# A state-space stage: constants loaded in an earlier block, and two GpSimd products given to VectorE

## The chip, the cores and the metric

One core of one Trainium2 chip runs the whole program. The time is the device time of one execution in microseconds. TensorE (PE; its weight loads are PEld) multiplies into PSUM, VectorE (DVE), ScalarE (ACT) and GpSimd (POOL) work on tiles in SBUF, and transfers are issued from the queues of SyncE (SP), ACT and POOL. Each engine runs its own instructions in order and waits at an instruction until what it needs is there.

## The reference, cut to what matters

The input is 512 tokens of 1024 columns. Two layers of a first block (a gated short convolution beside a rotary retention) come first; then 16 meta tokens are put ahead, and a state-space layer (SSD), an MLP, an attention layer and another MLP follow, 528 tokens each. Of the state-space layer, with 32 heads in 8 groups and chunks of 128 tokens:

```python
z, xbc, dt = jnp.split(h @ w_in, ...)
xbc = jax.nn.silu(causal_depthwise_conv_2(xbc, conv_w, conv_b))
dt = jax.nn.softplus(dt + dt_bias)
a = -jnp.exp(a_log)
a_cs = jnp.cumsum(dt * a)                            # in each chunk
y_diag = einsum(cb * exp(a_cs_l - a_cs_s), x * dt)   # in a chunk
y_off = einsum(c * exp(a_cs), state before the chunk)
g = rms_norm((y + x * d_skip) * silu(z)) * norm_g    # in each group
out = g @ w_out
```

All is float32. To keep its precision a product is made of three matmuls: each factor is a high part (a cast, by ACT) and a low part (the rest, by DVE or POOL).

## The kernel before, in words

**Weights.** `Stream` (lines 27 to 78) loads all weights in one order, 1 MB of 1024 rows and 256 columns at a time, from SP's queue into `wraw`, of which there are two. ACT casts four pieces of it to `whi` (line 65) and DVE subtracts to get `wlo` (line 66); there are two of each. A weight's `whi` buffer comes free when TensorE has done the weight two places before it, so ACT can cast the next weight only while TensorE works on the one in between. In the first block TensorE works a weight off in 11.1 us.

**First block, convolution half** (from line 455). For each of four parts p the weights come in the order c, x, b, z. DVE takes the sums out of PSUM (`cR` for c and x, `t` for b, `s` for z), ACT makes silu of `s`, DVE `t*s`, and `split` (line 247) forms the high part `mh_c` (ACT) and the low part `ml_c` (DVE) of the mixed tile.

**State-space stage** (from line 659). Its pool `sp` takes the SBUF space of the first block's pool. Before its first weight stand its constants: `dcol` (two transfers of 64x16 single floats, each 8 bytes behind the last, line 665), `e1`, `dtb` (line 672) and `ea` (line 674), all transfers from POOL's queue, and exp(`ea`) on ACT (line 675). The taps of its convolution are halved in `vec` on DVE (line 691). `steps` (line 692) makes dt and the running sums; only its line 722 reads `ea`. Then, for each of 8 groups, five chunks c: `cb` and `M` (DVE, lines 798 and 804), the decayed C `eb` (exp on ACT, line 810, times C on POOL, line 811), matmuls with `M` (line 818) and `eb` (line 820), the states `pv` (POOL line 833, DVE line 834) and the gated tile `gz` (DVE line 839, POOL line 841). At a group's end `gz` is normed (line 879) and split; the low part `ml_s` is POOL's in groups 0 to 6, DVE's in group 7 (line 881). The matmuls of the next weights stand between those of a chunk.

**Order.** A scheduler orders each engine's instructions when the program is built, by its own estimate of when each could start; it moves them across the statements of the source, as long as what they depend on allows. So an instruction's place in the source isn't its place on its engine.

Of the kernel before, what the change touches and what calls it, by code (L numbers as in the profile page):

```python
# [9 lines left out]
F32 = mybir.dt.float32  # L10
# [3 lines left out]
AF = mybir.ActivationFunctionType  # L14
ALU = mybir.AluOpType
PSUM = bass.MemoryType.PSUM

P = 128
# [3 lines left out]
T2 = SEQ + META  # L22
# [57 lines left out]
def build(ctx, tc, a):  # L80
    nc = tc.nc
    V = nc.vector
# [108 lines left out]
    cols = cp.tile([P, 4], F32, name="cols")  # L191
    Rx = cp.tile([P, T2], F32, name="Rx")
    vec = cp.tile([P, 3 * P], F32, name="vec")
    xres = cp.tile([P, 8, T2], F32, name="xres")
    V_PRE, V_POST, V_CW, V_LNM, V_LNF = 0, 16, 32, 80, 96
    V_SCW, V_SCB, V_SNG, V_QA, V_KVA = 128, 256, 288, 304, 307
# [51 lines left out]
    def split(dst, src, cs, eng=V):  # L248
        h, l = dst
        nc.scalar.copy(h[:, cs], src)  # L250
        eng.tensor_tensor(l[:, cs], src, h[:, cs].bitcast(F32), ALU.subtract)
# [31 lines left out]
    with ExitStack() as c1:  # L283
# [171 lines left out]
        for l in range(2):  # L455

            mixc = []
            for p in range(4):
                cR = [tmp(f"cR{l}{p}{n}") for n in range(2)]
                if p == 0:  # L460
                    for _, os_, u, pss in duo([(l, "c", 0), (l, "x", 0)], X, META, load_x if l == 0 else None):
                        for n in range(2):
                            V.tensor_tensor(cR[n][:, os_], pss[n], (RR, cR[n])[u][:, os_], ALU.mult)
                else:
                    for n, ps in dense((l, "c", p), X):
                        V.tensor_tensor(cR[n], ps, RR, ALU.mult)
                    for n, ps in dense((l, "x", p), X):
                        V.tensor_tensor(cR[n], ps, cR[n], ALU.mult)
                ts = []
                for n in range(2):  # L470
                    j = 2 * p + n
                    u = cR[n]
                    t = tmp(f"t{l}{j}")
                    wc = [gcol(V_CW, (l * 3 + q) * 8 + j) for q in range(3)]
                    nc.scalar.activation(t, u, AF.Identity, scale=wc[2])
                    V.scalar_tensor_tensor(t[:, 1:], u[:, :-1], wc[1], t[:, 1:], ALU.mult, ALU.add)
                    V.scalar_tensor_tensor(t[:, 2:], u[:, :-2], wc[0], t[:, 2:], ALU.mult, ALU.add)
                    ts.append(t)
                for n, ps in dense((l, "b", p), X):
                    V.tensor_tensor(ts[n], ps, ts[n], ALU.mult)  # L480
                    V.tensor_tensor(ts[n], ts[n], R, ALU.mult)
                for n, ps in dense((l, "z", p), X):
                    s = tmp(f"s{l}{p}{n}")
                    V.tensor_tensor(s, ps, R, ALU.mult)
                    nc.scalar.activation(s, s, AF.Silu)
                    V.tensor_tensor(ts[n], ts[n], s, ALU.mult)
                    m = mix_tile(f"c{l}{p}{n}")
                    split(m, ts[n], MS)
                    mixc.append(m)
                if l == 0 and p == 0:  # L490
                    late_vectors()
                    rotary_tables()
                if p == 3:
                    c_ = tmp(f"crot{l}")
                    nc.sync.dma_start(c_, rot[0])
                    V.tensor_tensor(CR, c_, R, ALU.mult)
                    s_ = tmp(f"srot{l}")
                    nc.sync.dma_start(s_, rot[1])
                    V.tensor_tensor(SR, s_, R, ALU.mult)

                    for b in range(4):
                        nc.tensor.transpose(C0[:, P * b : P * b + P], R[:, P * b : P * b + P], ident)
                    V.tensor_copy(Rt, C0[:, 0 : 4 * P : P])
# [148 lines left out]
    with ExitStack() as c2:  # L652
# [7 lines left out]
        small = {n: sp.tile([P, 5, 32], F32, name=n) for n in ("dt", "acs", "wd", "cdec")}  # L660
        dt, acs, wd, cdec = (small[n] for n in ("dt", "acs", "wd", "cdec"))
        acsD = tc.dram_tile([32, T2], F32, name="acsD")
        dcol = sp.tile([P, 16], F32, name="dcol")
        for i in range(2):
            nc.gpsimd.dma_start(
                dcol[64 * i : 64 * i + 64, :],
                a["ssd_d_2"][0].rearrange("(j two) -> two j", two=2)[i : i + 1].partition_broadcast(64))
        e1 = sp.tile([P, 32], F32, name="e1")
        V.memset(e1, 0.0)
        V.memset(e1[:, 0:1], 1.0)  # L670
        dtb = sp.tile([32, 1], F32, name="dtb")
        nc.gpsimd.dma_start(dtb, a["ssd_dt_bias_2"].rearrange("o h -> h o"))
        ea = sp.tile([P, 32], F32, name="ea")
        nc.gpsimd.dma_start(ea, a["ssd_a_log_2"].partition_broadcast(P))
        nc.scalar.activation(ea, ea, AF.Exp)
        def conv_silu(ps, j, tag, name):

            u = tmp(f"u{name}")
# [9 lines left out]
            V.scalar_tensor_tensor(t, u, 1.0, t, ALU.add, ALU.mult)  # L688
            return t

        V.tensor_scalar(vec[:, V_SCW : V_SNG + 16], vec[:, V_SCW : V_SNG + 16], 0.5, None, ALU.mult)
        def steps():

            w = ws.next("dt")
            ps = acc2()[:, :, :HW]
            mm3([(ps[:32, i], HS[i]) for i in range(2)], w, slice(0, 32), X, 8)
            dT = tmp("dT")[:32]
            V.tensor_tensor(halves(dT), ps[:32], halves(Rx)[:32], ALU.mult)
            nc.scalar.activation(dT, dT, AF.Identity, bias=dtb)
            for c, (t0, W) in enumerate(CH):  # L700
                nc.tensor.transpose(D0[:W, 32 * c : 32 * c + 32], dT[:, t0 : t0 + W], ident[:32, :32])
            f = [tmp(f"sf{i}", "sz", 3)[:, :160] for i in range(3)] + [tmp("sf3", "rb", 1)[:, :160]]
            x_, e_, s_, q_ = f
            V.memset(x_[:, :32], 0.0)
            V.tensor_copy(x_[:META, :32], D0[:META, :32])
            V.tensor_copy(x_[:, 32:], D0[:, 32:160])
            V.scalar_tensor_tensor(e_, x_, -1.0, x_, ALU.mult, ALU.max)
            nc.scalar.activation(e_, e_, AF.Exp, scale=-1.0)

            V.tensor_scalar(s_, e_, 2.0, None, ALU.add)  # L710
            V.reciprocal(s_, s_)
            V.tensor_tensor(s_, s_, e_, ALU.mult)
            V.tensor_tensor(e_, s_, s_, ALU.mult)
            V.tensor_scalar(q_, e_, 1.0 / 17.0, None, ALU.mult)
            for n in range(15, 1, -2):
                V.scalar_tensor_tensor(q_, q_, 1.0 / n, e_, ALU.add, ALU.mult)
            V.scalar_tensor_tensor(q_, q_, 1.0, s_, ALU.add, ALU.mult)
            V.tensor_scalar(x_, x_, 0.0, None, ALU.max)
            dtf = dt.rearrange("p c h -> p (c h)")
            V.scalar_tensor_tensor(dtf, q_, 2.0, x_, ALU.mult, ALU.add)  # L720
            V.tensor_scalar(dt[:, 0], dt[:, 0], cols[:, 2:3], None, ALU.mult)
            V.scalar_tensor_tensor(e_.rearrange("p (c h) -> p c h", c=5), dt, -1.0,
                                   ea.unsqueeze(1).to_broadcast([P, 5, 32]), ALU.mult, ALU.mult)
            cs_ps = D0
            nc.tensor.matmul(cs_ps[:, :160], tri, e_, start=True, stop=True)
            nc.tensor.matmul(cs_ps[:, 160:320], ones, e_, start=True, stop=True)
            acf, wdf, cdf = (t.rearrange("p c h -> p (c h)") for t in (acs, wd, cdec))
            V.tensor_copy(acf, cs_ps[:, :160])
            V.tensor_tensor(wdf, cs_ps[:, 160:320], acf, ALU.subtract)
            nc.scalar.activation(wdf, wdf, AF.Exp)  # L730
            V.tensor_tensor(wdf, wdf, dtf, ALU.mult)
            nc.scalar.activation(cdf, cs_ps[:, 160:320], AF.Exp)
            aT = tmp("aT")[:32]
            for c, (t0, W) in enumerate(CH):
                tp = (D0, D1)[c % 2][:32, :W]
                nc.tensor.transpose(tp, acs[:W, c, :], ident[:W, :W])
                V.tensor_copy(aT[:, t0 : t0 + W], tp)
            nc.gpsimd.dma_start(acsD, aT)
# [19 lines left out]
        for g in range(8):  # L758
# [24 lines left out]
            for c, (t0, W) in enumerate(CH):  # L783
# [24 lines left out]
                if c > 0:  # L808
                    eb = sp.tile([P, 4, P], F32, tag="eb", name=f"eb{nm}", bufs=2)
                    nc.scalar.activation(eb, ab, AF.Exp)  # L810
                    nc.gpsimd.tensor_tensor(eb, eb, Cs[:, ts_].unsqueeze(1).to_broadcast([P, 4, P]), ALU.mult)
                for n in range(2):
                    for cross in range(2 if c > 0 else 1):
                        for i in range(2):
# [63 lines left out]
            for n in range(2):  # L878
                V.scalar_tensor_tensor(gz[n], gz[n], gcol(V_SNG, 2 * g + n), rb, ALU.mult, ALU.mult)
                m = mix_tile(f"s{g}{n}")  # L880
                split(m, gz[n], slice(0, T2), nc.gpsimd if g < 7 else V)
                mix.append(m)
        Xn, sums = out_pass(2, mix)
        X = Xn
# [82 lines left out]
    with c4:  # L967
# [55 lines left out]
        for i in range(2):  # L1023
            o = side[i][:3, :HW]
# [359 lines left out]
```

## Time and profile before

| | |
|---|---|
| time, median of 3 runs (lowest to highest) | 2577.65 us (2577.57 to 2577.69) |
| profiled execution, its own time | 2570.25 us |
| its span | 2568.5 us |
| PE busy | 2502.8 us, 97% |
| DVE busy | 1476.5 us, 57% |
| ACT busy | 996.3 us, 39% |
| POOL busy | 258.1 us, 10% |
| mean granted clock of TensorE | 0.993 |

Busy is the time in which an engine had at least one instruction in work; matmuls overlap, so TensorE's busy share says little about its pace. The page's slices show TensorE at nine tenths or more nearly throughout; the slice from 1027 to 1092 us is at seven tenths, and there alone the granted clock falls to 0.7. That is the start of the state-space stage, which lasts to about 1538 us.

### The profile page before, as it was taken

What the parts mean: (1) busy time and instruction counts of PE and PEld (TensorE: products, weight loads), DVE (VectorE), ACT (ScalarE), POOL (GpSimd) and SP (SyncE); (2) the same over time, 40 slices, a digit from 0 to 9 for tenths busy, and PEclk for the clock granted to TensorE, in tenths of its full rate; (3) what the DMA queues carried; (4) which work ended last, traced back from release to release, by engine and by line L of the source; (5) the groups of instructions that cost most, each with busy time, mean ns of one, the idle gap of its engine ahead of it and who ended that gap; (6) DMA issues with size and microseconds to landing.
All of it is one profiled execution on the core that took longest, in us unless ns stands there. A gap on an engine that the chain in (4) does not pass through costs nothing.

```text
span 2568.5 us, 40249 instructions
## 1 busy us (share of the span) xinstructions
PE 2502.8 (97%) x16657; PEld 2212.7 (86%) x16657; DVE 1476.5 (57%) x2844; ACT 996.3 (39%) x2162; POOL 258.1 (10%) x254
## 2 busy tenths in 40 slices
PE   8999999999999999799999999999999999999999
PEld 7888888888888888699999999999997666799898
DVE  6743555564435456588848875434455765644443
ACT  4322333432223344365535543323335764423321
POOL 1000000100000002153413430000011000100000
PEclk9999999999999999799999999999999999999999
DMA  4333222223332321433333223232322121223322
GB/s 141 107 99 107 66 83 88 76 71 96 107 94 78 91 81 54 64 100 95 94 96 93 79 82 106 83 99 83 99 69 71 52 61 43 90 85 96 99 91 74
DMA packets 213383, 220.88 MB, mean 86 GB/s; under 512 B 8796, under 2 KB 203469, under 8 KB 213200
## 3 DMA queue, kind: packets, MB, share of 16 engines
q1 hardware_dynamic: 208512, 207.50, 26.4%
q0 software_dynamic: 4208, 10.68, 2.4%
q8 instruction: 130, 2.13, 0.3%
q14 instruction: 53, 0.43, 0.1%
q10 hardware_dynamic: 480, 0.13, 0.0%
HBM read 215.46 MB, written 2.83 MB: 85 GB/s over the span
## 4 chain that ended last, share of the span: by engine, by line
PE 89%; DVE 4%; ACT 3%; DMA 1%; POOL 1%; issue 1%; POOLq 0%; ACTq 0%; DVEq 0%
PE pb L222 57%; PE main L222 10%; PE main L229 8%; PE pb L229 4%; PE side L1217 1%; PE side L1230 1%; PE side L818 1%; DMA ea<-ssd_a_log 1%; PE main L1223 1%; PE side L827 1%; POOL sums L260 1%; DVE wlo L66 1%; PE side L543 1%; PE side L561 1%; DVE M L804 1%
## 5 line engine op out<-in xcount | busy, mean ns | idle before, releaser
L65 ACT CAST whi<-wraw 128x512 fp32r<-128x512 f32 (+2 forms) x721 | 408.0, 621 | 906.3 <-PE pb L222 567.2
L66 DVE TENSOR_TENSOR wlo<-wraw,whi 128x512 fp32r<-128x512 f32 (+2 forms) x721 | 491.3, 722 | 192.7 <-ACT whi L65 191.7
L222 PE MATMUL pb<-xh_n,whi 128*128 128x264 f32 (+3 forms) x1264 | 348.6, 325 | 16.7 <-ACT whi L65 13.9
L222 PE MATMUL pb<-xh_n,wlo 128*128 128x264 f32 (+3 forms) x1264 | 357.3, 328 | 0.0
L222 PE MATMUL pb<-xl_n,whi 128*128 128x264 f32 (+3 forms) x1264 | 349.1, 325 | 0.0
L222 PEld LDWEIGHTS pb<-xh_n,whi 128*128 128x128 f32 (+1 forms) x1264 | 215.5, 190 | 35.9 <-ACT whi L65 14.1
L222 PEld LDWEIGHTS pb<-xh_n,wlo 128*128 128x128 f32 (+1 forms) x1264 | 216.6, 190 | 20.6 <-issue 2.6
L222 PEld LDWEIGHTS pb<-xl_n,whi 128*128 128x128 f32 (+1 forms) x1264 | 214.8, 190 | 17.7
L222 PE MATMUL pb<-xh_l,whi 128*128 128x512 f32 (+1 forms) x480 | 183.5, 383 | 4.2 <-ACT whi L65 3.0
L222 PE MATMUL pb<-xl_l,whi 128*128 128x512 f32 (+1 forms) x480 | 184.1, 384 | 0.8 <-DVE xl_l L215 0.8
L222 PE MATMUL pb<-xh_l,wlo 128*128 128x512 f32 (+1 forms) x480 | 183.4, 382 | 0.0
L229 PE MATMUL main<-whi,mh_w 128*128 128x256 f32 x512 | 144.4, 282 | 0.1
L229 PE MATMUL main<-whi,ml_w 128*128 128x256 f32 x512 | 143.5, 281 | 0.0
L229 PE MATMUL main<-wlo,mh_w 128*128 128x256 f32 x512 | 143.5, 281 | 0.0
L222 PEld LDWEIGHTS pb<-xh_l,whi 128*128 128x128 f32 x480 | 90.6, 189 | 22.9 <-ACT whi L65 3.4
L222 PEld LDWEIGHTS pb<-xl_l,whi 128*128 128x128 f32 x480 | 90.8, 189 | 18.5 <-DVE xl_l L215 1.2
L222 PEld LDWEIGHTS pb<-xh_l,wlo 128*128 128x128 f32 x480 | 90.9, 189 | 17.2
L222 PE MATMUL pb<-xh_m,whi 128*128 128x264 f32 x512 | 104.5, 285 | 0.1
L222 PE MATMUL pb<-xl_m,whi 128*128 128x264 f32 x512 | 104.4, 285 | 0.0
L222 PE MATMUL pb<-xh_m,wlo 128*128 128x264 f32 x512 | 104.3, 285 | 0.0
L222 PE MATMUL pb<-ml_u,whi 128*128 128x264 f32 x512 | 103.9, 284 | 0.0
L222 PE MATMUL pb<-mh_u,wlo 128*128 128x264 f32 x512 | 103.9, 284 | 0.0
(542 smaller groups left out, 5616.8 us busy)
## 6 DMA issues: line engine op xcount, KB each, us to landing
wraw<-w_in SPq DMA_DIRECT2D x64, 1024.0 KB, 5.9
wraw<-mlp_w_up SPq DMA_DIRECT2D x32, 1024.0 KB, 5.5
wraw<-mlp_w_down SPq DMA_DIRECT2D x32, 1024.0 KB, 4.9
wraw<-w_out SPq DMA_DIRECT2D x16, 1024.0 KB, 4.9
wraw<-ssd_w_in SPq DMA_DIRECT2D x16, 1024.0 KB, 5.2
wraw<-ssd_w_in SPq DMA_DIRECT2D x16, 512.0 KB
ab<-acsD POOLq DMA_DIRECT2D x32, 256.0 KB, 3.8
wraw<-ssd_w_out SPq DMA_DIRECT2D x5, 1024.0 KB
```

The source lines that it names most:

```text
L65: nc.scalar.copy(hv[s], rv[s])
L66: eng.tensor_tensor(lv[s], rv[s], hv[s].bitcast(F32), ALU.subtract)
L222: nc.tensor.matmul(ps, w[wq][:, k, wsl], x(xq, k, cs), start=(k == 0 and wq + xq == 0), stop=(k == nk - 1 and wq == 1))
L229: nc.tensor.matmul(ps, x(xq, k, ts_), w[wq][:, k, csl], start=(k == 0 and wq + xq == 0), stop=(k == nk - 1 and xq == 1))
L260: nc.gpsimd.tensor_tensor(dst, dst, v, ALU.add)
L543: nc.tensor.matmul(ch(A, c), ch(kT, c), ch(qT, c), start=True, stop=True)
L561: nc.tensor.matmul(ch(op, c), ch(pm, c), v[:, c, P * n : P * n + P], start=True, stop=(c == 0))
L804: V.tensor_tensor(M[:W, :, :W], M[:W, :, :W], cb[:W, :W].unsqueeze(1).to_broadcast([W, 4, W]), ALU.mult)
L818: nc.tensor.matmul(o, xd[:W, h], M[:W, h, :W], start=True, stop=(c == 0))
L827: nc.tensor.matmul(st[:, :256], Bt[:W], xw[:W].rearrange("p h e -> p (h e)"), start=True, stop=True)
L1217: nc.tensor.matmul(sp_, Qh[:, h, q0 : q0 + M], Kh[:, h, :L], start=True, stop=False)
L1223: nc.tensor.transpose(pst[:, c, :M], p[:M, P * c : P * c + P], ident[:M, :M])
```

## The change

Three edits, on lines of the kernel before. The tiles `dcol`, `e1`, `dtb` and `ea` are taken from the pool that lives through the whole program, and are filled in the first block, layer 0, at the end of part p = 1, together with the halving of the taps. Three small DVE copies of the tile `t` (here `ts[0]`) into `dcol`, `ea` and `dtb` stand ahead of their transfers, which so can't begin before `t` is there. The exp of `ea` is now a statement of `steps`. The product of `eb` is given to DVE, and so is the low part `ml_s` in groups 0 to 6.

```diff
--- before.py
+++ after.py
@@ -191,6 +191,10 @@
     cols = cp.tile([P, 4], F32, name="cols")
     Rx = cp.tile([P, T2], F32, name="Rx")
     vec = cp.tile([P, 3 * P], F32, name="vec")
+    dcol = cp.tile([P, 16], F32, name="dcol")
+    e1 = cp.tile([P, 32], F32, name="e1")
+    dtb = cp.tile([32, 1], F32, name="dtb")
+    ea = cp.tile([P, 32], F32, name="ea")
     xres = cp.tile([P, 8, T2], F32, name="xres")
     V_PRE, V_POST, V_CW, V_LNM, V_LNF = 0, 16, 32, 80, 96
     V_SCW, V_SCB, V_SNG, V_QA, V_KVA = 128, 256, 288, 304, 307
@@ -487,6 +491,19 @@
                     m = mix_tile(f"c{l}{p}{n}")
                     split(m, ts[n], MS)
                     mixc.append(m)
+                if l == 0 and p == 1:
+
+                    for t, n in ((dcol, P), (ea, P), (dtb, 32)):
+                        V.tensor_copy(t, ts[0][:n, : t.shape[-1]])
+                    V.memset(e1, 0.0)
+                    V.memset(e1[:, 0:1], 1.0)
+                    V.tensor_scalar(vec[:, V_SCW : V_SNG + 16], vec[:, V_SCW : V_SNG + 16], 0.5, None, ALU.mult)
+                    for i in range(2):
+                        nc.gpsimd.dma_start(
+                            dcol[64 * i : 64 * i + 64, :],
+                            a["ssd_d_2"][0].rearrange("(j two) -> two j", two=2)[i : i + 1].partition_broadcast(64))
+                    nc.gpsimd.dma_start(dtb, a["ssd_dt_bias_2"].rearrange("o h -> h o"))
+                    nc.gpsimd.dma_start(ea, a["ssd_a_log_2"].partition_broadcast(P))
                 if l == 0 and p == 0:
                     late_vectors()
                     rotary_tables()
@@ -660,19 +677,6 @@
         small = {n: sp.tile([P, 5, 32], F32, name=n) for n in ("dt", "acs", "wd", "cdec")}
         dt, acs, wd, cdec = (small[n] for n in ("dt", "acs", "wd", "cdec"))
         acsD = tc.dram_tile([32, T2], F32, name="acsD")
-        dcol = sp.tile([P, 16], F32, name="dcol")
-        for i in range(2):
-            nc.gpsimd.dma_start(
-                dcol[64 * i : 64 * i + 64, :],
-                a["ssd_d_2"][0].rearrange("(j two) -> two j", two=2)[i : i + 1].partition_broadcast(64))
-        e1 = sp.tile([P, 32], F32, name="e1")
-        V.memset(e1, 0.0)
-        V.memset(e1[:, 0:1], 1.0)
-        dtb = sp.tile([32, 1], F32, name="dtb")
-        nc.gpsimd.dma_start(dtb, a["ssd_dt_bias_2"].rearrange("o h -> h o"))
-        ea = sp.tile([P, 32], F32, name="ea")
-        nc.gpsimd.dma_start(ea, a["ssd_a_log_2"].partition_broadcast(P))
-        nc.scalar.activation(ea, ea, AF.Exp)
         def conv_silu(ps, j, tag, name):
 
             u = tmp(f"u{name}")
@@ -688,7 +692,6 @@
             V.scalar_tensor_tensor(t, u, 1.0, t, ALU.add, ALU.mult)
             return t
 
-        V.tensor_scalar(vec[:, V_SCW : V_SNG + 16], vec[:, V_SCW : V_SNG + 16], 0.5, None, ALU.mult)
         def steps():
 
             w = ws.next("dt")
@@ -697,6 +700,7 @@
             dT = tmp("dT")[:32]
             V.tensor_tensor(halves(dT), ps[:32], halves(Rx)[:32], ALU.mult)
             nc.scalar.activation(dT, dT, AF.Identity, bias=dtb)
+            nc.scalar.activation(ea, ea, AF.Exp)
             for c, (t0, W) in enumerate(CH):
                 nc.tensor.transpose(D0[:W, 32 * c : 32 * c + 32], dT[:, t0 : t0 + W], ident[:32, :32])
             f = [tmp(f"sf{i}", "sz", 3)[:, :160] for i in range(3)] + [tmp("sf3", "rb", 1)[:, :160]]
@@ -808,7 +812,7 @@
                 if c > 0:
                     eb = sp.tile([P, 4, P], F32, tag="eb", name=f"eb{nm}", bufs=2)
                     nc.scalar.activation(eb, ab, AF.Exp)
-                    nc.gpsimd.tensor_tensor(eb, eb, Cs[:, ts_].unsqueeze(1).to_broadcast([P, 4, P]), ALU.mult)
+                    V.tensor_tensor(eb, eb, Cs[:, ts_].unsqueeze(1).to_broadcast([P, 4, P]), ALU.mult)
                 for n in range(2):
                     for cross in range(2 if c > 0 else 1):
                         for i in range(2):
@@ -878,7 +882,7 @@
             for n in range(2):
                 V.scalar_tensor_tensor(gz[n], gz[n], gcol(V_SNG, 2 * g + n), rb, ALU.mult, ALU.mult)
                 m = mix_tile(f"s{g}{n}")
-                split(m, gz[n], slice(0, T2), nc.gpsimd if g < 7 else V)
+                split(m, gz[n], slice(0, T2))
                 mix.append(m)
         Xn, sums = out_pass(2, mix)
         X = Xn
```

**ACT, first block, parts 1 and 2.** What stands there before, from the casts of the mixed tiles of p = 1 (`whi_1048` are the weights b of p = 2, `whi_1118` those of z):

```order
L485 ACTIVATE s_976<-s_976 128x512
L65 CAST whi_986<-wraw_988 128x512
L250 CAST mh_c_972<-t_836 128x512
L250 CAST mh_c_980<-t_840 128x512
L65 CAST whi_1048<-wraw_1050 128x512 x4
L65 CAST whi_1118<-wraw_1120 128x512 x2
```

And now, where `whi_1062` are the weights b of p = 2, `whi_1132` those of z:

```order
L489 ACTIVATE s_980<-s_980 128x512
L65 CAST whi_1000<-wraw_1002 128x512
L254 CAST mh_c_976<-t_840 128x512
L254 CAST mh_c_984<-t_844 128x512
L703 ACT_TABLE_LOAD
L703 ACTIVATE ea<-ea 128x32
L65 CAST whi_1062<-wraw_1064 128x512 x4
L65 CAST whi_1132<-wraw_1134 128x512 x2
```

The exp of `ea`, which stands in `steps` in the source, is placed on ACT right behind the casts of p = 1, with a table load, ahead of the casts of the next weights.

**ACT, start of the state-space stage.** Before (`whi_7839` are the weights of B and C of group 0):

```order
L269 ACTIVATE Rx<-side_73,eps 128x256
L682 ACTIVATE xs_7775<-uxs_7773,vec 128x528
L65 CAST whi_7839<-wraw_7841 128x512
L675 ACT_TABLE_LOAD
L675 ACTIVATE ea<-ea 128x32
L682 ACTIVATE xs_7832<-uxs_7830,vec 128x528
L65 CAST whi_7839<-wraw_7841 128x512 x2
```

And now (there `whi_7841`):

```order
L273 ACTIVATE Rx<-side_73,eps 128x256
L686 ACTIVATE xs_7777<-uxs_7775,vec 128x528
L65 CAST whi_7841<-wraw_7843 128x512 x2
L686 ACTIVATE xs_7834<-uxs_7832,vec 128x528
L65 CAST whi_7841<-wraw_7843 128x512 x2
L691 ACT_TABLE_LOAD
```

`ea` has gone from there, and all four casts stand before the first instruction that needs the table.

**DVE, chunks 2 to 4 of group 0, now.** The same rows stood there before without the two of `eb`:

```order
L808 TENSOR_TENSOR M_2_8274<-M_2_8274,cb_2_8272 128x512
L827 TENSOR_TENSOR xw_2_8294<-side_72,wd 128x256
L815 TENSOR_TENSOR eb_3_8323<-eb_3_8323,Cs_8075 128x512
L843 SCALAR_TENSOR_TENSOR gz_8200<-xs_7777,dcol,side_70 128x272
L843 SCALAR_TENSOR_TENSOR gz_8201<-xs_7834,dcol,side_71 128x272
L838 TENSOR_TENSOR pv_2_8299<-side_73,pv_2_8299 128x256
L802 TENSOR_TENSOR cb_3_8312<-side_72,tri 128x128
L811 TENSOR_TENSOR xd_3_8321<-side_72,dt 128x256
L808 TENSOR_TENSOR M_3_8314<-M_3_8314,cb_3_8312 128x512
L827 TENSOR_TENSOR xw_3_8334<-side_72,wd 128x256
L815 TENSOR_TENSOR eb_4_8358<-eb_4_8358,Cs_8075 128x512
L683 TENSOR_TENSOR uxs_8476<-pb_78,Rx 128x528
```

The products of chunks 3 and 4 stand behind `xw` of the chunk before; those of chunks 1 and 2 stand ahead of chunk 0. The halving of the taps stands on DVE where it stood, in the first block, since the scheduler had put it there already.

## Rows read from the trace of the kernel before

**Rows 1.** The chain that ended last: start us, length us, what.
```profile
1031.59 1.84 POOL dcol L665 x2
1033.94 20.65 DMA ea<-ssd_a_log
1056.12 4.12 PE pb L222 x17
1114.22 23.81 PE pb L222 x194
```

**Rows 2.** Timeline of ACT: start, length, instruction, [idle before, releaser].
```profile
1035.87 1.28 ACT L675 ACT_TABLE_LOAD   x1
1054.61 0.23 ACT L675 ACTIVATE ea<-ea 128x32 f32<-128x32 f32 x1 [17.46 <-DMA ea<-ssd_a_log]
```

**Rows 3.** Timeline of PE, the same stretch.
```profile
1056.12 0.81 PE L222 MATMUL pb<-xh_n,whi 128*128 128x264 f32 x2 [13.89 <-ACT whi L65]
...
1073.38 0.43 PE L725 MATMUL side<-sf,tri 128*128 128x160 f32 x2
```

**Rows 4.** Windows: us, busy PE, PEld, DVE, ACT, POOL, granted clock, DMA.
```profile
1044.00:1045.00 1.00, 0.00 (x0) 0.00 (x0) 0.00 (x0) 0.00 (x0) 0.00 (x0) 0.75 3.58 2
1068.00:1069.00 1.00, 1.00 (x9) 1.00 (x8) 0.91 (x3) 0.00 (x0) 0.00 (x0) 0.80 0.89 259
1078.00:1079.00 1.00, 1.00 (x9) 0.99 (x9) 0.98 (x3) 1.00 (x2) 0.00 (x0) 0.82 0.00 0
1082.00:1083.00 1.00, 1.00 (x10) 1.00 (x9) 1.00 (x3) 0.65 (x2) 1.00 (x3) 0.97 0.19 14
```

**Rows 5.** Timeline of DVE, start of the state-space stage.
```profile
1062.58 0.18 DVE L705 COPY sf<-side 16x32 f32<-16x32 f32 x1 [0.32 <-PE side L701]
...
1070.73 0.33 DVE L722 SCALAR_TENSOR_TENSOR sf<-dt,ea 128x160 f32<-128x160 f32 x1
```

**Rows 6.** Timeline of ACT, first block, parts 1 and 2.
```profile
118.25 1.14 ACT L250 CAST mh_c<-t 128x512 fp32r<-128x512 f32 x2
124.82 2.18 ACT L65 CAST whi<-wraw 128x512 fp32r<-128x512 f32 x4 [5.44 <-issue]
```

**Rows 7.** Timeline of DVE, the same stretch.
```profile
117.86 0.69 DVE L486 TENSOR_TENSOR t<-t,s 128x512 f32<-128x512 f32 x1 [0.35 <-ACT s L485]
...
136.13 1.29 DVE L468 TENSOR_TENSOR cR<-pb,cR 128x512 f32<-128x512 f32 x2 [7.43 <-PE pb L222]
```

**Rows 8.** Timeline of SP's queue, the same stretch.
```profile
121.63 0.37 SPq L57 DMA_DIRECT2D wraw<-w_in  x1
```

**Rows 9.** Transfers issued from 100 to 180 us: KB each, median us to landing.
```profile
wraw<-w_in SPq DMA_DIRECT2D x7, 1024.0 KB, 6.5
```

**Rows 10.** POOL's groups: count | busy us, mean ns | idle before, releasers.
```profile
L811 POOL TENSOR_TENSOR eb<-eb,Cs 128x512 f32<-128x512 f32 x32 | 47.7, 1499 | 25.2 <-DVE Cs L688 22.6 <-ACT eb L810 2.6
...
L251 POOL TENSOR_TENSOR ml_s<-gz,mh_s 128x528 fp32r<-128x528 f32 x14 | 25.9, 1869 | 31.9 <-ACT mh_s L250 31.9
```

**Rows 11.** DVE's groups by shape, 1100 to 1500 us.
```profile
L804 DVE TENSOR_TENSOR M<-M,cb 128x512 f32<-128x512 f32 x31 | 27.4, 885 | 0.1
```

**Rows 12.** DVE's group of the low part in group 7.
```profile
L251 DVE TENSOR_TENSOR ml_s<-gz,mh_s 128x528 fp32r<-128x528 f32 x2 | 1.4, 708 | 0.0
```

**Rows 13.** Timeline of DVE, chunks 2 to 4 of group 2.
```profile
1193.56 0.68 DVE L804 TENSOR_TENSOR M<-M,cb 128x512 f32<-128x512 f32 x1
...
1195.10 0.93 DVE L839 SCALAR_TENSOR_TENSOR gz<-xs,dcol,side 128x272 f32<-128x272 f32 x2 [0.52 <-PE side L820]
...
1197.24 2.74 DVE L804 TENSOR_TENSOR M<-M,cb 128x512 f32<-128x512 f32 x1
...
1201.97 0.42 DVE L834 TENSOR_TENSOR pv<-side,pv 128x256 f32<-128x256 f32 x1 [1.04 <-PE side L827]
```

**Rows 14.** Timeline of POOL, the same stretch.
```profile
1198.17 1.25 POOL L811 TENSOR_TENSOR eb<-eb,Cs 128x512 f32<-128x512 f32 x1
```

**Rows 15.** Waits of PE from 1100 to 1500 us: in total, times, longest.
```profile
PE side L818 <- DVE M L804: 6.3, 11, 1.9
```

## The prediction

> **What bounds the kernel now.** I read the page's slices first: TensorE is nine tenths busy nearly throughout, with one dent at the start of the state-space stage. Then the chain of waits there: the last link is not work but a transfer, `ea`, issued at 1033.94 and 20.65 us on its way, behind the two of `dcol` that began at 1031.59 [rows 1]. ACT's timeline shows who waits: the exp of `ea` stood idle for 17.46 us [rows 2], and behind it in ACT's queue stood the casts of the next weights. So TensorE, done at 1056.12 - 13.89 = 1042.23, had nothing until 1056.12 [rows 3]. The windows show the rest of the price: the granted clock fell to half about 2.3 us after TensorE stopped (0.75 over the window from 1044), stayed there until about 1068.4 (0.80 over that window), and dipped once more from about 1078.6 to 1082.1 [rows 4]. In the groups that follow, TensorE waits little: 6.3 us in eleven waits for `M` between 1100 and 1500 [rows 15].
>
> **Constants, at the start of the stage: what goes.** The idle 13.9 us go, since `ea` no longer stands ahead of the casts (the order of ACT shows it). From 1056.12 to 1073.38 [rows 3] TensorE did 82 of the 96 matmuls of B and C, and dT's transposes. At the pace of a full clock, 23.81/194 = 0.123 us each [rows 1], that is 10.1 us and some 0.4 for the transposes; it took 17.3. That would give 6.8 us more. But the chain of small DVE operations from dT's copy to `ea`'s product then becomes late. It took 1070.73 + 0.33 - 1062.58 = 8.5 us [rows 5], about 7.3 with the two casts' low parts that now stand outside it; it can start some 4.4 us after TensorE is done with dt (dT, its bias on ACT, transposes, three low parts ahead of it in DVE's queue), so it ends near 1042.2 + 11.7 = 1053.9, while TensorE gets there at 1042.2 + 10.5 = 1052.7. I take 1.2 us of new wait and a little for the start: 5.2 us of the 6.8. Sum: 13.9 + 5.2 = 19 us; at least 13.9 (nothing of the clock comes back), at most 20.7.
>
> **Constants, in the first block: what comes.** ACT's order has the exp right behind the casts of p = 1, with the transfer still ahead of it: what ACT waited for at 1037 it will wait for at 120. The DVE copies follow `t`, ready at 117.86 + 0.69 = 118.55 [rows 7], each priced by the 0.18 us of a small copy [rows 5]; POOL is idle there and issues at about 118.75. From the first issue of `dcol` to the exp of `ea` it took 1054.61 - 1031.59 = 23.0 us [rows 1, 2]; so `ea` is there at 141.7. What is queued behind it: the casts of the weights b of p = 2, which before ran at 124.82 [rows 6], on DVE their low parts, and behind those the sums `cR`. TensorE wants these weights when it is done with x; DVE's `cR` puts that at about 135.94 (it started at 136.13) [rows 7]. The first cast comes some 0.85 us after `ea`, at 142.6: an idle of 6.6 us, and so the wait is not taken away but moved to where the transfer has 17.2 us of cover from its first issue (118.75 to 135.94) instead of 10.6 (1031.59 to 1042.23).
>
> That was with no load beside it. Now a weight load of 1 MB starts at 121.63 [rows 8] and takes 6.5 us to land [rows 9]. Bounds: it adds nothing, or all its 6.5 us; idle 6.6 to 13.1. I take 1.5, so 8.1, nearer to the measured transfer, which is small in bytes. Below: the trace has no shorter one of this kind, and only one under 16 us would leave no idle; I keep that as a rival. Here the Trainium skill bears (DMA: Bandwidth & Descriptors, section SWDGE vs HWDGE vs iDMA): it says that a DMA engine changes between its queues only at the end of a packet, of at most 64 descriptors. By it `dcol`'s few long packets would hardly wait for the load, rather the load for them, and 1.5 us is even much; no run here shows it yet.
>
> The clock falls after such an idle, as it did 2.3 us into the other; it was down for 3.5 us in the dip (1078.6 to 1082.1), and for 12 us of resumed work after the long idle (1056.1 to 1068.4) [rows 4]. Half of that is lost: 2 to 6 us; I take 2.5, since TensorE has unbroken work there. Sum: 10.6 us lost; from 0 (no idle) to 19. The later casts catch up while TensorE works 11 us on each weight. Two table loads of 1.28 us [rows 2] come to ACT in the first block, beside its waits, at nothing; without that cover they would be 2.6 us. `e1`, `dtb` and the taps cost nothing: short DVE work, and the taps stay where the scheduler had them.
>
> **`eb` and `ml_s` on DVE.** POOL loses 32 x 1.50 and 14 x 1.87 us [rows 10]; it is not late in the stage except after DVE's `gz`. DVE gets 32 products like `M`, 0.68 us [rows 13], and 14 low parts of 0.71 [rows 12]: 21.8 + 9.9 = 31.7 us over eight groups. It gets something back: `M` takes 0.885 us on average [rows 11] where 0.68 would do, 31 x 0.2 = 6.4 us, and one of 2.74 us [rows 13] ends as POOL's `eb` does, at 1198.17 + 1.25 [rows 14]. The products of chunks 3 and 4 stand where DVE idled 0.52 and 1.04 us for TensorE [rows 13]; the cover just holds. Of TensorE's 6.3 us of waits for `M`, two long ones of 1.9 [rows 15] should go: I take 2.5 us gained, between 6.3 gained and 10 lost (0.3 us in each of 32 chunks where the cover doesn't hold).
>
> A rule that speaks against this edit is in the Trainium skill (SBUF — State Buffer, section Who interferes with whom): a DVE instruction with two SBUF inputs and a GpSimd instruction that reads SBUF exclude each other, and the one issued first wins. `M`'s 2.74 us agree. By it the moved products can in turn be held by POOL's `pv` and `gz`; that is the third rival.
>
> **Sum.** -19 + 10.6 - 2.5 = -10.9 us against the profiled execution's 2570.25 (2568.5 of span and 1.75 around it): 2559.35, a ratio of 0.9958. On the median of 2577.65, which is 0.3% above that execution, it is 2566.7 us.
>
> **Rivals.**
> 1. *No idle in the first block.* The transfer lands by 135, in 16 us instead of 23, because there neither the residual's POOL work nor a reused SBUF tile stands ahead of it. For it: TensorE has 17 us of cover from the issue. Against it: the chain names nothing but the transfer in those 20.65 us [rows 1], so it is slow by itself. -19 - 2.5 = -21.5: 2556 us.
> 2. *The whole wait again.* The load beside it stretches it to 30 us; idle 14 and clock 5: -19 + 19 - 2.5 = -2.5: 2575 us, no change that can be told. For it: the load's bytes use the same 16 engines.
> 3. *DVE becomes late in the chunks.* Place: `eb` of chunks 3 and 4 next to POOL's `gz` and `pv`; price 0.3 us in 32 chunks: -19 + 10.6 + 9.6 = +1.2: 2579 us, no change. For it: the 0.52 us of cover is less than the 0.68 of a product. Against it: `M`'s own delay goes.
> 4. *Slower.* One mechanism: single floats beside a weight load take twice the 23 us. `ea` comes at 164.7, TensorE idles 164.7 + 0.85 - 135.94 = 29.6 us and loses 5 to the clock: -19 + 34.6 - 2.5 = +13: 2591 us. It decides from where the idle is longer than 16.5 us, that is a transfer over 33 us. Against it: by the time the load has landed, at 128, three fifths of the transfer are still to come, unhindered.
>
> **How the numbers follow.** Forecast 0.55, rival 1 0.12, rival 2 0.13, rival 3 0.10, rival 4 0.10. A measurement of this kernel tells about 0.2%, 5.2 us, from no change. The forecast's own range, with the idle from 6.6 to 11 us and the chunks within 3 us of it, is 2561 to 2572, all faster; with rival 1 and a share of 0.03 of rival 2 that is 0.70 faster. The rest of rival 2 and most of rival 3 make 0.17 the same; rival 4 and the tail of rival 3 make 0.13 slower. The range for 8 in 10 takes in rival 1 nearly and rival 2: 2555 to 2577.
>
> **What the profile after would show.** Right: in ACT's timeline an idle of about 20 us ahead of `ea` near 121 us, released by its transfer; in PE's one of 7 to 9 us near 136, waiting for `whi`, and a window at half clock behind it; no idle of more than 2 us between 1030 and 1070 (shifted by the 10 us); `M` without lengths over 1.5 us. Wrong: no idle near 136 (rival 1), one over 16 us (rivals 2 and 4), or more than 6.3 us of waits for `M` or `eb` in the groups (rival 3).

## The result, and the profile after

| | before | changed |
|---|---|---|
| median of four runs, us | 2577.61 | 2561.73 (forecast 2566.7, range 2555 to 2577) |
| ratio, 95% interval | 1 | 0.9939 (0.9923 to 0.9954) |
| the profiled execution, us | 2570.25 | 2556.87 |

The change is faster by 0.6%, 15.9 us by the medians and 13.4 between the two profiled executions. Of the forecast cases it is the likeliest one, with one term too small.

First ACT's timeline of the changed kernel in the first block (start, length, instruction, idle before and its releaser), the answer to [rows 2, 6]:

```profile
142.83 0.23 ACT L703 ACTIVATE ea<-ea 128x32 f32<-128x32 f32 x1 [22.41 <-DMA ea<-ssd_a_log]
142.97 2.16 ACT L65 CAST whi<-wraw 128x512 fp32r<-128x512 f32 x4
147.87 1.15 ACT L65 CAST whi<-wraw 128x512 fp32r<-128x512 f32 x2 [2.74 <-DMA wraw<-w_in]
```

The wait for `ea` is there, 22.41 us long. The four casts that ran at 124.82 before stand behind it. PE's timeline, the answer to [rows 3]:

```profile
143.62 0.80 PE L226 MATMUL pb<-xh_l,whi 128*128 128x512 f32 x1 [7.79 <-ACT whi L65]
...
1063.19 0.54 PE L729 MATMUL side<-sf,tri 128*128 128x160 f32 x2 [0.63 <-DVE sf L726]
```

TensorE idles 7.79 us in the first block (8.1 forecast). At the start of the state-space stage it waits 0.63 us for the chain of small operations (1.2 forecast) and nowhere for weights, though 9.3 us late from the first block it is there 10.2 us earlier than in [rows 3]. Windows of the changed kernel (columns as in [rows 4]):

```profile
136.00:140.00 4.00, 0.00 (x0) 0.00 (x0) 0.00 (x0) 0.00 (x0) 0.00 (x0) 0.98 0.14 24
140.00:144.00 4.00, 0.38 (x1) 0.38 (x2) 0.40 (x1) 1.17 (x4) 0.00 (x0) 0.50 0.66 187
144.00:148.00 4.00, 4.00 (x13) 3.10 (x13) 3.30 (x6) 1.26 (x4) 0.00 (x0) 0.67 0.37 109
148.00:152.00 4.00, 4.00 (x19) 3.23 (x18) 3.02 (x5) 3.29 (x6) 0.00 (x0) 1.00 0.72 214
1068.00:1072.00 4.00, 4.00 (x23) 4.00 (x22) 3.98 (x8) 1.07 (x3) 0.53 (x1) 0.57 0.76 260
```

TensorE stopped at 143.62 - 7.79 = 135.83. The granted clock fell to half near 139.8 (0.98 over the window from 136), 4.0 us after the stop where it was 2.3 us in [rows 4], and stayed there for about 3 us of resumed work, which costs 1.5 us (2.5 forecast). The dip of [rows 4] from 1078.6 is still there, now from about 1068. Next the DMA view from 118 to 160 us, whose GB/s line has 40 slices of 1.05 us:

```profile
GB/s 0 0 1 1 2 0 0 0 0 0 0 0 1 2 0 0 0 0 2 30 61 105 182 253 210 134 51 62 196 214 367 171 0 0 0 109 194 215 356 125
q0 software_dynamic: 128, 0.02, 42.0%
dcol<-ssd_d POOLq DMA_DIRECT2D x2, 4.0 KB, 18.0
ea<-ssd_a_log POOLq DMA_DIRECT2D x1, 16.0 KB, 21.8
```

This I had not priced: the load of 1 MB issued at 121.59 moves hardly a byte until 138, while GpSimd's queue with `dcol` in it (q0: packets, MB, share of 16 engines) holds the engines for 42% of the window with 0.02 MB. The load lands near 147.8 instead of after the 6.5 us of [rows 9]. Here it costs nothing, since TensorE is late itself. Last PE's waits from 1100 to 1500 us, the answer to [rows 15]:

```profile
PE side L822 <- DVE M L808: 0.9, 2, 0.7
```

### The profile page after: what moved, and what is told of

The parts are those of the page before. It is cut to its first block, busy times and chain, and to the rows that moved or that the text cites. A ratio compares the mean times of both kernels' runs of the same rounds, so it can differ in the third digit from the quotient of the medians.

```text
span 2555.1 us, 40242 instructions
## 1 busy us (share of the span) xinstructions
PE 2500.3 (98%) x16657; PEld 2209.6 (86%) x16657; DVE 1480.3 (58%) x2893; ACT 1001.2 (39%) x2164; POOL 182.6 (7%) x208
## 4 chain that ended last, share of the span: by engine, by line
PE 86%; DVE 5%; ACT 3%; issue 3%; DMA 2%; POOL 1%; POOLq 0%; ACTq 0%; DVEq 0%
PE pb L226 53%; PE main L226 10%; PE main L233 8%; PE pb L233 4%; PE side L1221 1%; PE side L1234 1%; DMA ea<-ssd_a_log 1%; DVE wlo L66 1%; PE side L822 1%; PE main L1227 1%; PE side L831 1%; POOL sums L264 1%; PE side L560 1%; PE side L578 1%; PE side L580 1%
## 5 line engine op out<-in xcount | busy, mean ns | idle before, releaser
L66 DVE TENSOR_TENSOR wlo<-wraw,whi 128x512 fp32r<-128x512 f32 (+2 forms) x721 | 483.1, 711 | 209.6 <-ACT whi L65 208.5
L226 PEld LDWEIGHTS pb<-xh_n,wlo 128*128 128x128 f32 (+1 forms) x1264 | 214.6, 188 | 19.4 <-issue 1.4
L226 PEld LDWEIGHTS pb<-xh_l,whi 128*128 128x128 f32 x480 | 91.1, 190 | 31.3 <-ACT whi L65 11.8
L226 PE MATMUL pb<-mh_u,whi 128*128 128x264 f32 x512 | 103.7, 284 | 0.0
```

What stands on the lines that cost most here:

```text
L66: eng.tensor_tensor(lv[s], rv[s], hv[s].bitcast(F32), ALU.subtract)
L226: nc.tensor.matmul(ps, w[wq][:, k, wsl], x(xq, k, cs), start=(k == 0 and wq + xq == 0), stop=(k == nk - 1 and wq == 1))
```

## The experiments

Four stretches tell the parts of the time apart in each trace. *Block 1*: the start of the first matmul from `sqp`, at the end of the first block. *Start*: from the last matmul from `sqp` to the first of `sf` with `tri`. *Loop*: from there to the first of `gq` with `ones` in group 7. *M*: TensorE's waits for `M` from 1080 to 1490. "Long" counts the waits of 1.9 us among them. The ratio is of 4 to 12 executions of each kernel against 4 to 20 of the kernel before, the rest is of one trace.

| kernel | ratio, 95% | block 1 | start | loop | M | long |
|---|---|---|---|---|---|---|
| before | 1 | 498.4 | 55.5 | 418.1 | 6.3 | 2 |
| before, second profile (e12) | 0.9999 (0.9985 to 1.0014) | 498.0 | 55.6 | 426.9 | 11.8 | 5 |
| changed | 0.9939 (0.9923 to 0.9954) | 507.7 | 35.8 | 414.2 | 0.9 | 0 |
| constants alone (e1) | 0.9969 (0.9956 to 0.9983) | 509.0 | 35.8 | 422.1 | 8.4 | 3 |
| VectorE edits alone (e2) | 0.9967 (0.9955 to 0.9979) | 498.2 | 55.3 | 412.2 | 0.6 | 0 |
| `eb` alone (e9) | 0.9973 (0.9962 to 0.9984) | 498.4 | 54.3 | 419.1 | 4.0 | 0 |
| `ml_s` alone (e10) | 1.0000 (0.9988 to 1.0011) | 497.7 | 55.3 | 421.8 | 8.4 | 4 |
| changed, one `dcol` behind `ea` (e3) | 0.9913 (0.9898 to 0.9929) | 505.1 | 37.3 | 413.7 | 1.8 | 0 |
| changed, exp late (e4) | 0.9925 (0.9910 to 0.9940) | 503.3 | 35.8 | 414.1 | 2.0 | 0 |
| changed, `dcol` twice (e6) | 0.9993 (0.9983 to 1.0003) | 522.7 | 35.8 | 415.0 | 1.8 | 0 |
| changed, D as rows (e5) | 0.9891 (0.9874 to 0.9908) | 498.1 | 37.3 | 414.1 | 2.0 | 0 |
| VectorE edits, D as rows at its old place (e8) | 0.9894 (0.9877 to 0.9910) | 498.9 | 37.6 | 411.7 | 1.1 | 0 |
| before, D as rows (e11) | 0.9927 (0.9909 to 0.9945) | 498.3 | 36.1 | 423.2 | 11.6 | 5 |
| before, `ea` first (e7) | 0.9955 (0.9937 to 0.9973) | 500.1 | 44.5 | 421.6 | 9.7 | 4 |

**e1 and e2: the two halves.** e1 is the changed kernel with these two lines as before; e2 is the kernel before with them changed.

```diff
-  V.tensor_tensor(eb, eb, Cs...)
+  nc.gpsimd.tensor_tensor(eb, eb, Cs...)
-  split(m, gz[n], slice(0, T2))
+  split(m, gz[n], slice(0, T2), nc.gpsimd if g < 7 else V)
```

> The constants alone are moved; decayed C and the low parts of the gated tiles stay on GpSimd as before. My theory (constants -9 to -10 us net, the rest from the chunk loop): the mark at the end of block 1 and the idle near 136 as in the changed kernel, the first dT-sum matmul of the state-space stage about 10 us earlier than before, but from there to the end of the group loop the same length as before, with TensorE's waits for M again about 6 us; total about 10 us less than before, ratio about 0.996. Rival (the two VectorE edits are worth nothing and the gain in the loop is the clock's or the shift's): as the changed kernel, ratio 0.994.

> Only decayed C and the low parts are moved to VectorE; the constants stay at the start of the state-space stage. My theory: 17 us of wait for ea stay as before, the group loop is 3 to 4.5 us shorter, TensorE's waits for M fall from 6.3 us to about 1; total -3 to -4 us, ratio 0.9985. Rival (VectorE late in the chunks): up to +10 us, waits for M of over 10 us. Rival (the edits need the constants' change to pay): no change within 1 us.

e1: the constants bring 0.31%, 8 us; block 1 is 10.6 us later, the start 19.7 shorter, and the loop is not shorter. e2: the products bring 0.33%, 8.5 us by the runs, over twice what I expected, though only 3.7 between its profiled execution and that of before. That gap is taken up at e12.

**e9 and e10: which of the two edits.** Each is the kernel before with one of the two lines above.

> The kernel before with only decayed C (32 products) moved to VectorE; the low parts of the gated tiles stay on GpSimd. My theory: TensorE's waits for M come from GpSimd's product beside M, so this edit carries nearly all of the loop's gain: waits for M from 6.3 us to below 2, the loop 3 to 4 us shorter, total -3 to -7 us (the two edits together measured a ratio of 0.9967). Rival (the low parts carry it): waits for M of over 4 us stay, total within 1.5 us of before.

> The kernel before with only the 14 low parts of the gated tiles moved to VectorE; decayed C stays on GpSimd. My theory: TensorE does not wait for these low parts, so nothing: waits for M stay at 5 to 8 us, the loop within 1 us of before, total within 1.5 us. Rival (the low parts carry the gain of the two edits): waits for M fall below 3 us, -3 to -7 us.

`eb` carries it; `ml_s` alone is worth nothing that can be told from zero. DVE's groups of `M` from 1100 to 1500 us (count, busy us, mean ns), first with `ml_s` alone on VectorE, then with `eb` alone:

```profile
L804 DVE TENSOR_TENSOR M<-M,cb 128x512 f32<-128x512 f32 x31 | 30.9, 997 | 0.0
```

```profile
L804 DVE TENSOR_TENSOR M<-M,cb 128x512 f32<-128x512 f32 x31 | 24.3, 784 | 0.1
```

What makes the mean 997 ns are products of 2.75 us. Two timelines of e10, DVE's and POOL's, show one:

```profile
1384.66 0.68 DVE L804 TENSOR_TENSOR M<-M,cb 128x512 f32<-128x512 f32 x1
1388.32 2.75 DVE L804 TENSOR_TENSOR M<-M,cb 128x512 f32<-128x512 f32 x1
```

```profile
1387.22 1.51 POOL L841 TENSOR_TENSOR gz<-gz,sz 128x272 f32<-128x272 f32 x2
1388.68 0.62 POOL L833 TENSOR_TENSOR pv<-pv,cdec 128x256 f32<-128x256 f32 x1
1389.26 1.26 POOL L811 TENSOR_TENSOR eb<-eb,Cs 128x512 f32<-128x512 f32 x1
```

The same product took 0.68 us one chunk earlier. Here it starts while GpSimd's `gz` is at work and ends 0.55 us after `eb` does, at 1388.32 + 2.75 = 1391.07: it was held through the end of `gz`, `pv` and `eb`. The matmul that needs it waited 1.93 us. The exclusion that the Trainium skill states (SBUF — State Buffer, Who interferes with whom) agrees. My expectation for e9 missed the wait: 4.0 us stayed where I expected under 2, in five waits of at most 1.13 us, but with none of 1.9.

**e12: the kernel before, profiled a second time.**

> The kernel before, unchanged, profiled a second time. In the five traces so far with decayed C on GpSimd, TensorE waits 1.92 us for M two, three, four, four and five times in the group loop, and 0.2 us in the other groups; the loop (from the first matmul of the dt sums to the first of group 7's norm) was 418.1 us where it was two, and 421.6 to 423.2 where it was more; the kernel before was the one with two. My theory (which of the two products goes first is decided anew in each group and execution, and the first profile drew few): again 2 to 5 of them, the same kernel at another number; loop about 418 us if two, 421 to 424 if four or five. Rival (the number belongs to the kernel): exactly two, at the same groups (near 1200 and 1391), loop 418 us.

Five long waits, and at other places; a loop of 426.9 us, longer than I expected for five; a time of 2578.64. PE's timeline of this execution, in five of its groups:

```profile
1106.40 0.44 PE L818 MATMUL side<-M,xd 128*64 128x128 f32 x4 [1.93 <-DVE M L804]
...
1154.89 0.44 PE L818 MATMUL side<-M,xd 128*64 128x128 f32 x4 [1.93 <-DVE M L804]
...
1205.73 0.44 PE L818 MATMUL side<-M,xd 128*64 128x128 f32 x4 [1.93 <-DVE M L804]
...
1348.16 0.44 PE L818 MATMUL side<-M,xd 128*64 128x128 f32 x4 [0.24 <-DVE M L804]
...
1396.93 0.44 PE L818 MATMUL side<-M,xd 128*64 128x128 f32 x4 [1.92 <-DVE M L804]
```

The wait is 1.9 us or about 0.24, and which one is decided anew in each group and execution. What differs is who goes first when `gz` ends. In the group with 0.24, DVE's and POOL's timelines:

```profile
1347.25 0.85 DVE L804 TENSOR_TENSOR M<-M,cb 128x512 f32<-128x512 f32 x1
```

```profile
1347.41 1.16 POOL L833 TENSOR_TENSOR pv<-pv,cdec 128x256 f32<-128x256 f32 x1
```

There `M` went first, and `pv` took 1.16 us instead of 0.62. In the six traces with `eb` on GpSimd, 23 of the 48 groups are of the long kind and 18 of this one; in the other 7 `pv` starts first. In both of these kinds `M` starts 0.16 to 0.45 us ahead of `pv`, so the order of their starts, by which the prediction had the first win, doesn't tell which one goes; what does stays open. With `eb` on VectorE `M` can still be held by `pv`, but no second product follows on GpSimd.

Behind some of the long waits the clock falls for a few us; windows of the same execution:

```profile
1204.00:1212.00 8.00, 6.27 (x51) 5.67 (x52) 5.39 (x10) 2.77 (x9) 2.61 (x3) 0.79 0.29 72
1396.00:1400.00 4.00, 3.07 (x25) 2.79 (x26) 2.42 (x5) 2.41 (x8) 1.29 (x3) 0.79 0.30 67
```

A dip costs about (1 - 0.79) x 8 = 1.7 us. Besides the one at the loop's start that both have, this execution has three in the loop and the first profile had one. Three more long waits at 1.93 - 0.24 and two more dips make 3 x 1.7 + 2 x 1.7 = 8.5 us; the loops differ by 8.8. So the profile that I read before predicting was a favourable one, and with `eb` on VectorE no long wait is left to be drawn: none of the eight such traces has one. Dips remain, since they come behind shorter waits too. The changed kernel has one in its loop, behind a wait for `M` of 0.71 us at 1130.70:

```profile
1132.00:1136.00 4.00, 4.00 (x22) 3.67 (x21) 3.53 (x8) 2.32 (x7) 1.38 (x2) 0.64 0.10 8
```

Most traces have one or more outside the loop as well, not at the same places (near 1530 us in e1 and e2, near 2120 in before and e1).

Together the two account for the loops. Taking from each loop its waits for `M` and what the half clock cost in it (each window's length times one minus its granted clock) leaves 408.2 to 410.4 us in 13 of the 14 traces. In e7, where TensorE comes into the loop out of a long wait and at half clock, it leaves 405.8.

**e5: D as rows, in block 1.**

```diff
-  for i in range(2):
-      nc.gpsimd.dma_start(dcol[64*i : 64*i+64, :], ssd_d_2[0].rearrange(...)[i : i+1].partition_broadcast(64))
+  nc.gpsimd.dma_start(db, ssd_d_2.partition_broadcast(P))
   ...
+  for i in range(2):
+      V.tensor_copy(dcol[64*i : 64*i+64, :], db[64*i : 64*i+64, i::2])
```

> The changed kernel with D loaded as one broadcast of 128 rows of 128 bytes into an own tile, from which two small copies of VectorE pick the even and the odd columns into dcol; the same values without transfers of single floats. My theory (cost goes by the number of single floats): D and ea land within about 4 us, the load issued at 121.6 is not held and lands in about 6.5 us as before, no idle at 136 and full clock there: about 9.5 us less than the changed kernel, near 0.990 of before. Rival (any partition broadcast from GpSimd's queue is slow): idle at 136 as in the changed kernel. Rival (block 1 has other costs than the idle): idle gone, but less than half of the 9.5 us gained.

As expected: block 1 is back at 498.1, and between the profiled executions it is 2556.87 - 2547.59 = 9.3 us faster than the changed kernel. ACT's timeline, then issues from 118 to 160 us:

```profile
124.49 0.23 ACT L703 ACTIVATE ea<-ea 128x32 f32<-128x32 f32 x1 [4.07 <-DMA ea<-ssd_a_log]
```

```profile
db<-ssd_d POOLq DMA_DIRECT2D x1, 16.0 KB, 3.3
dtb<-ssd_dt_bias POOLq DMA_DIRECT2D x1, 0.1 KB, 2.8
ea<-ssd_a_log POOLq DMA_DIRECT2D x1, 16.0 KB, 4.6
```

D now moves 16 KB instead of 8, and `ea` lands after 4.6 us instead of 21.8.

**e3: `ea` and `dtb` issued ahead of `dcol`** (the statements in the other order).

> The changed kernel with the small transfers of ea and dtb issued ahead of the two of dcol. My theory (the wait for ea is time queued behind dcol's 2,048 single floats, not ea's own): ea lands in 2 to 4 us, by about 125; no wait of ACT for it beyond some 3 us, no idle of TensorE at 136 and no half clock there: 8 to 9.5 us less than the changed kernel, were it not that the weight load issued at 121.6 is still held behind dcol until about 138 to 148, so that TensorE, now on time, may wait for the next weights near 147 by 1 to 3 us. Total 6 to 9 us less than the changed kernel. Rival 1 (the broadcast of ea is slow by itself): ea lands about 20 us after its issue, idle at 136 as in the changed kernel. Rival 2 (a held load stalls the whole of the next stage): the idle at 136 is replaced by one of over 6 us near 147, no gain.

`ea` did not land in 2 to 4 us, because the order that ran was another: one `dcol`, `dtb`, `ea`, the other `dcol`. That gave a middle step instead. Landing of `ea`, from the view of its issues:

```profile
ea<-ssd_a_log POOLq DMA_DIRECT2D x1, 16.0 KB, 13.2
```

With none, one and two transfers of single floats ahead of it: 4.6, 13.2, 21.8 us, 8.6 for each. The idle at 136 was gone, yet block 1 gained only 2.6 us, for the held load now showed, with a dip of the clock behind it (0.92 from 152 to 156 us, 0.65 from 156 to 160):

```profile
149.47 0.51 PE L226 MATMUL pb<-xh_l,whi 128*128 128x512 f32 x1 [2.57 <-ACT whi L65]
153.99 0.50 PE L226 MATMUL pb<-xh_l,wlo 128*128 128x512 f32 x1 [2.14 <-DVE wlo L66]
```

**e4: the exp tied to the residual's scale**, so that it runs at the start of the stage while the transfers stay in block 1.

```diff
-  nc.scalar.activation(ea, ea, AF.Exp)
+  zc = sp.tile([P, 1], F32, name="zc")
+  V.tensor_scalar(zc, Rx[:, 0:1], 0.0, None, ALU.mult)
+  nc.scalar.activation(ea, ea, AF.Exp, bias=zc)
```

> The changed kernel, but the exp of ea is tied to the residual's scale and so runs at the start of the state-space stage; the transfers stay in block 1. My theory has two costs in block 1, ACT blocked by the exp (7.8 us of idle) and the 1 MB weight load of 121.6 held behind dcol until about 148. Here the first goes and the second stays: no idle at 136, but TensorE waits near 147 for the held weights, in all 3 to 6 us, as with ea between the two transfers of dcol; mark at the end of block 1 5 to 7 us later than before; total 3 to 5 us below the changed kernel. Rival (only ACT's block costs): mark within 1 us of before, 9 to 10 us below the changed kernel.

Block 1 is 4.9 us late, not within 1: two waits of 2.1 us at the same matmuls as in e3, here without a dip. ACT's block and the held load are two costs, and taking away the first uncovers the second. The total came out only 1.4 us below the changed kernel by the profiled executions, less than expected: behind the loop this trace has three dips (near 1522, 1938 and 2068 us) and that of the changed kernel one. The ratios' intervals overlap.

**e6: `dcol`'s two transfers issued twice.**

> The changed kernel with dcol's two transfers issued twice (the same values land twice). So far ea took 4.6, 13.2 and 21.8 us from issue to landing with none, one and two transfers of single floats ahead of it. My theory (they queue up, 8.6 us for each): 39 us with four, ea's exp near 162, TensorE idle 26 to 28 us near 136, the mark at the end of block 1 about 28 to 32 us later than before. Rival (a fixed delay in which transfers overlap): ea within 25 us, idle under 12 us.

Not what I meant to build: the second pair writes the same tile, so it waited for the first and was issued behind `ea`, which landed as before. It measured the held load instead, with two more transfers issued while it waited. POOL's timeline, then PE's:

```profile
132.62 0.84 POOL L506 DMA_DIRECT2D dcol<-ssd_d  x1 [10.65 <-DMA dcol<-ssd_d]
143.17 0.82 POOL L506 DMA_DIRECT2D dcol<-ssd_d  x1 [9.71 <-DMA dcol<-ssd_d]
```

```profile
144.93 0.79 PE L226 MATMUL pb<-xh_l,whi 128*128 128x512 f32 x1 [8.73 <-ACT whi L65]
166.68 0.80 PE L226 MATMUL pb<-xh_l,whi 128*128 128x512 f32 x1 [8.95 <-ACT whi L65]
```

The same 1 MB now lands near 166, and TensorE idles a second time; block 1 is 15 us later than in the changed kernel and the whole gain is lost.

**e7: the kernel before, `ea` and `dtb` issued first at their old place.**

> The kernel before, with one edit: the transfers of dtb and ea are issued ahead of the two of dcol at the start of the state-space stage; nothing is moved to block 1 or to VectorE. My theory: ea lands 4 to 5 us after its issue, the 13.9 us of idle at 1042 go with the half clock behind, about 19 us, less what the weight loads held behind dcol cost there (0 to 6 us): 13 to 19 us less than before, as much as or more than the whole change gains. Rival (ea's own transfer is slow at this place, behind the residual's GpSimd work): idle over 8 us stays, gain under 8 us.

`ea` landed in 3.1 us and the idle of 13.9 went, but the start gained 11.0 us and not 13 to 19. ACT's and PE's timelines say why:

```profile
1061.68 2.18 ACT L65 CAST whi<-wraw 128x512 fp32r<-128x512 f32 x4 [10.52 <-DMA wraw<-ssd_w_in]
```

```profile
1064.06 0.90 PE L725 MATMUL side<-sf,tri 128*128 128x160 f32 x2 [7.40 <-DVE sf L722]
```

And DVE's:

```profile
1062.33 0.69 DVE L66 TENSOR_TENSOR wlo<-wraw,whi 128x512 fp32r<-128x512 f32 x1 [5.48 <-ACT whi L65]
```

A weight load, issued at 1047.32 behind `dcol`, moved next to nothing until about 1052 and came late; DVE's queue stood behind that weight's low part, and the chain to `sf` behind it. Against the start of e11, where nothing holds the load, the cost is 44.5 - 36.1 = 8.4 us, above my 0 to 6.

**e8 and e11: D as rows, nothing moved.** The rows of e5 at the place of before, with the two VectorE edits (e8) and without (e11).

> The constants stay at the start of the state-space stage, as before, but D is loaded there as 128 rows of 128 bytes and picked apart by two small copies; decayed C and the low parts are on VectorE. My theory (the 17.5 us wait was dcol's single floats queued ahead of ea, so the place did not matter, the form of the transfer did): ea lands some 4 to 5 us after its issue, TensorE's 13.9 us of idle at 1042 and the half clock behind it go, about 19 us, and 3 to 4 us in the group loop: about 22 us less than before, within 3 us of the kernel with the rows in block 1. Rival (place matters too: the residual's GpSimd work delays the issue, or the stage's start needs the cover of a whole block): ACT still waits over 5 us for ea, TensorE idles, and the time is 5 us or more above the rows in block 1.

> The kernel before with one edit: D is loaded at its old place as 128 rows of 128 bytes and picked apart by two small copies; nothing else moves. My theory: the whole 18 to 21 us of the stage's start go, ratio 0.992 to 0.993, more than the constants' move gained (0.9969), and the loop keeps its 6 to 8 us of waits for M. Rival (the rows pay only together with the VectorE edits): under 12 us.

e8 equals e5 within 0.6 us between the profiled executions, and both beat the two kernels: with D as rows the place did not matter, the form of the transfer did. ACT's timeline of e8 has the exp 3.9 us after `ea`'s issue at 1034.83, with no wait:

```profile
1038.77 0.23 ACT L673 ACTIVATE ea<-ea 128x32 f32<-128x32 f32 x1
```

e11 changes only how D is loaded and already gains 0.73%, more than the whole change in its point estimate; its loop keeps five long waits.

## Why the prediction was right, and where it was not

- *The idle at the stage's start goes, with its clock: -19.* Shown: 55.5 to 35.8 is 19.7, the same in e1, and 19.4 in e11, which takes the wait away where it stood.
- *The wait moves to block 1: +10.6.* Shown, at +9.3 (10.6 in e1): idle 7.79 for 8.1, clock 1.5 for 2.5. The exp came 24.1 us after the first issue, 23.0 + 1.5 forecast. That `dcol` would not suffer from the load, but the load from it, held; the sum gave that no price. It had none only because ACT's block covered it, as e3, e4 and e7 show.
- *Copies, table loads, taps: nothing.* No wait of TensorE near 136 or at the stage's start is put down to them. The forecast's 118.75 for the first issue has room for one copy of 0.18 us and not for three; in the trace the three start 0.08 us apart and the issue came at 118.69, so nothing hung on it.
- *`eb` and `ml_s` on VectorE: -2.5.* This is the mis-sized term. By the runs the constants are worth -8.0 (e1; forecast -19 + 10.6 = -8.4) and the products -8.5 (e2; -11.6 to -5.4), together -16.5 where the whole change measured -15.9 (-19.8 to -11.9). Between the two profiled executions alone the loop gained 4.0 us, near the forecast. But the five traces of the loop with both on GpSimd (before, e12, e1, e7, e11) have a mean of 422.4, the seven with both on VectorE 413.6: -8.8, and the waits for `M` in them 9.6 and 1.5. That is beyond my bound of 6.3, which was TensorE's waits for `M` in one execution with two long ones, where two to five is what such an execution has; dips of the clock come on top. With these stretches the terms are -19.7 + 9.3 - 8.8 = -19.2, within the interval of the runs.
- *Rivals.* 1 and 2 fell by the 7.8 us of idle, 3 by `M`'s 0.9 us, 4 by the transfer's 24.1 us.

The step from the profiled execution to the median, by a ratio, took the 7.4 us between 2570.25 and 2577.65 as spread over the kernel. e12's 8.4 us of difference are not: nearly all are long waits and dips in this loop. But the changed kernel, with no long wait left, has such a step too: its profiled execution took 2556.87 us, the other three 2561.65 to 2562.27, at a mean granted clock of 0.993 to 0.995 against 0.996. That speaks for more half clock in those; where in the kernel, and how many long waits each unprofiled execution of before had, is not visible.

The e9 trace is a draw as well. Its loop is 3.3 us shorter than that mean of 422.4, while its runs gained 7 us. Against e2's it has 3.4 us more of waits for `M` (4.0 and 0.6) and 3.4 more lost to the half clock (5.1 and 1.7), nearly all of the 6.9 us between the two loops.

## What to carry to other kernels

Before moving a late transfer to an earlier place, see what stands ahead of it in its queue and in what pieces it moves: here two transfers of 1,024 single floats were the wait, and rewriting them as rows of 128 bytes was worth more than moving them, which also held up the weights of the other queue. A wait that appears at two lengths in equal groups is a draw; price it from several executions, or by its worst, not by the one profile at hand. Where a wait is covered by another, taking the other away uncovers it, so count both.

## What the runs showed of the hardware

- A transfer of 1,024 single floats from GpSimd's queue takes 8.6 us of that queue's time, while 16 KB in rows of 128 bytes landed 3.3 us after their issue.
- A 1 MB load from SP's queue, issued behind two such transfers, landed after 26 us instead of 6.5, and in e6, where two more were issued while it waited, after 44. The rule of the Trainium skill that the prediction weighed (DMA: Bandwidth & Descriptors, SWDGE vs HWDGE vs iDMA: a switch between queues only at a packet's end) agrees.
- A DVE product that started while GpSimd was at work took 1.05 us when it went next, and 2.75 when two more GpSimd instructions (0.62 and 1.26 us) went ahead of it, though it had started before both.
- A wait of TensorE of 1.9 us was followed by a few us of half clock at some places and not at others. Such dips, of 1.7 us each, also came behind waits of 0.7 to 1.1 us.
